# RMSNorm with each row repeated: another order of stores and loads on the DMA queue, wide copies, and the last tile undivided

## The chip, the core and the metric

The kernel runs on one core of a Trainium2 chip. The metric is the device time of one execution in microseconds (us), of which the median over several runs is taken. The kernel before took 240.07 us, the median of 5 runs between 239.79 and 240.6.

A core has several engines that run side by side, each with its own list of instructions. Four matter here: ScalarE (ACT in the profile), VectorE (DVE), GpSimd (POOL), and SyncE (SP), which here only issues transfers. All transfers between the large memory (HBM) and the on-chip memory (SBUF, 128 partitions) are carried by 16 DMA engines.

## What is computed

```python
def reference(x, gamma):            # x: (8, 512, 2048) f32, gamma: (2048,) f32
    x_rep = np.repeat(x, 2, axis=1)
    rms = np.sqrt((x_rep ** 2).mean(axis=-1, keepdims=True) + 1e-6)
    x_norm = x_rep / rms
    return (x_norm * gamma[None, None, :]).astype(np.float32)
```

Each of the 4096 rows is divided by the root of its mean square, multiplied by gamma and written out twice in succession. 33.55 MB are read and 67.11 MB are written.

## The kernel before, in words

The 4096 rows are cut into eight tiles of 512 rows (`ntiles` is 8). In a tile each of the 128 partitions holds `K = 4` successive input rows, which become 8 output rows. So a load is 4 MB (32 KB in each partition) and a store is 8 MB (64 KB in each partition), and both are contiguous in HBM within a partition.

**One buffer for input and output.** The buffer `y` of a tile has eight rows in each partition. The load (`load`, line 52) puts the four input rows into rows 4 to 7. Input row k is then scaled into row 2k, and a copy puts the same values into row 2k + 1. The pool `rows` has three such buffers, so tile i uses the buffer of tile i - 3, and load i cannot be issued until store i - 3 has landed.

**The work on a row.** `square` has ScalarE square the row and sum it up (line 64; the squares go to a throw-away tile in PSUM) and take the root (line 68). `scale` has VectorE take the reciprocal (line 73) and multiply the row by it and by gamma in one instruction (line 74). `repeat` copies one row (line 80). In `compute` the copies of all rows of a group but the last are ScalarE's, and that of the last row is VectorE's. On ScalarE the square of row k + 1 stands ahead of the copy of row k.

**The order of the work.** `tc.manual_schedule()` is entered: each engine's instructions stand in the order in which the program gives them. Every load and every store is issued by SP, which takes them one after the other and stands still at the first whose condition is not met. The order on SP is: load 0 in two halves, loads 1 and 2, stores 0 and 1, loads 3 and 4, stores 2 and 3, loads 5 and 6, stores 4 and 5, load 7 in two halves, store 6, store 7 in two halves. The last tile is both computed and stored by halves (`parts` in lines 108 to 111), and its load is halved as well (line 116).

**Gamma.** Four transfers of 2 KB, issued by ScalarE (line 98), bring gamma into one partition, and GpSimd copies it to all 128 (line 101). The first multiplication of line 74 needs that.

Of the kernel before, what the change touches and what calls it, by code (L numbers as in the profile page):

```python
# [1 line left out]

# [4 lines left out]


@with_exitstack
def kernel(  # L10
    ctx: ExitStack,
    tc: tile.TileContext,
    x: bass.AP,
    gamma: bass.AP,
    out: bass.AP,
):
    nc = tc.nc
    P = nc.NUM_PARTITIONS
    f32 = mybir.dt.float32
    Act = mybir.ActivationFunctionType  # L20
    Alu = mybir.AluOpType

    B, S, D = x.shape
    Bo, So, Do = out.shape
    R = So // S
    assert R == 2 and D == Do and B == Bo and So == S * R
    eps = 1e-6
    inv_d = 1.0 / float(D)


    K = 4
    N = B * S
    assert N % (P * K) == 0
    ntiles = N // (P * K)
    x_t = x.rearrange("b s d -> (b s) d").rearrange("(n p k) d -> n p k d", p=P, k=K)
    out_t = out.rearrange("b s d -> (b s) d").rearrange("(n p j) d -> n p (j d)", p=P, j=K * R)

    singles = ctx.enter_context(tc.tile_pool(name="singles", bufs=1))
    rows = ctx.enter_context(tc.tile_pool(name="rows", bufs=3))
    junk = ctx.enter_context(tc.tile_pool(name="junk", bufs=1, space=bass.MemoryType.PSUM))  # L40
    small = ctx.enter_context(tc.tile_pool(name="small", bufs=8))

    ys = []

    def load(i, eng, parts=1):


        y = rows.tile([P, K * R, D], f32, name="y")
        step = K // parts
        for k in range(0, K, step):  # L50
            at = K * (R - 1) + k
            eng.dma_start(out=y[:, at : at + step, :], in_=x_t[i, :, k : k + step, :])  # L52
        ys.append(y)

    def store(i, k0, k1):
        nc.sync.dma_start(  # L56
            out=out_t[i, :, R * k0 * D : R * k1 * D],
            in_=ys[i][:, R * k0 : R * k1, :].rearrange("p j d -> p (j d)"),
        )

    def square(i, k):
        sq = junk.tile([P, D], f32, name="sq")
        ss = small.tile([P, 1], f32, name="ss")
        nc.scalar.activation(  # L64
            out=sq[:], in_=ys[i][:, K * (R - 1) + k, :], func=Act.Square, accum_out=ss[:]
        )
        rms = small.tile([P, 1], f32, name="rms")
        nc.scalar.activation(out=rms[:], in_=ss[:], func=Act.Sqrt, scale=inv_d, bias=eps_t[:])  # L68
        return rms

    def scale(i, k, rms):
        rstd = small.tile([P, 1], f32, name="rstd")
        nc.vector.reciprocal(out=rstd[:], in_=rms[:])  # L73
        nc.vector.scalar_tensor_tensor(  # L74
            out=ys[i][:, R * k, :], in0=ys[i][:, K * (R - 1) + k, :], scalar=rstd[:], in1=gamma_b[:],
            op0=Alu.mult, op1=Alu.mult,
        )

    def repeat(i, k, copy):
        copy(out=ys[i][:, R * k + 1, :], in_=ys[i][:, R * k, :])  # L80

    def compute(i, k0, k1):

        rms = square(i, k0)
        for k in range(k0, k1):
            scale(i, k, rms)
            if k + 1 < k1:
                rms = square(i, k + 1)
                repeat(i, k, nc.scalar.copy)
            else:  # L90
                repeat(i, k, nc.vector.tensor_copy)


    ctx.enter_context(tc.manual_schedule())
    load(0, nc.sync, parts=2)
    gamma_b = singles.tile([P, D], f32, name="gamma_b")
    for c in range(0, D, D // 4):
        nc.scalar.dma_start(
            out=gamma_b[0:1, c : c + D // 4], in_=gamma[c : c + D // 4].partition_broadcast(1)
        )  # L100
    nc.gpsimd.partition_broadcast(out_ap=gamma_b[:], in_ap=gamma_b[0:1, :])  # L101
    eps_t = singles.tile([P, 1], f32, name="eps_t")
    nc.vector.memset(eps_t, eps)  # L103
    load(1, nc.sync)
    load(2, nc.sync)

    for i in range(ntiles):
        parts = 2 if i == ntiles - 1 else 1
        for k in range(0, K, K // parts):
            compute(i, k, k + K // parts)  # L110
            store(i, k, k + K // parts)

        if i % 2 == 1:
            for j in (i + 2, i + 3):
                if j < ntiles:
                    load(j, nc.sync, parts=2 if j + 1 == ntiles else 1)


# [1 line left out]
_INS = ['x', 'gamma']  # L120
_OUTS = [((8, 1024, 2048), 'float32')]


# [23 lines left out]
```

## Time and profile before

| | us |
|---|---|
| median of 5 runs | 240.07 |
| the profiled execution, its own time | 240.18 |
| its span, from the first instruction to the last | 238.4 |
| outside the span (the difference) | 1.78 |
| ScalarE busy | 115.4 |
| VectorE busy | 90.8 |
| GpSimd busy | 2.5 |

| line, engine, work | number | mean ns of one |
|---|---|---|
| 64, ACT, square of a row, 128x2048 | 32 | 1871 |
| 64, ACT, reading the sum | 32 | 187 |
| 68, ACT, root | 32 | 296 |
| 73, DVE, reciprocal | 32 | 162 |
| 74, DVE, row by reciprocal and gamma | 32 | 2352 |
| 80, ACT, copy of a row | 23 | 1890 |
| 80, DVE, copy of a row | 9 | 1227 |

Times within the profile are counted from the start of the span. A group's row gives the busy time of its instructions and the mean of one. The DMA share is the mean busy share of the 16 DMA engines in a stretch; since a packet is counted where it starts, a short stretch can show more than 1 or much less. The chain of waits is followed backwards from the end, from each step to what released it. An engine that is idle costs nothing as long as it is not the one that sets the end.

### The profile page before, as it was taken

The numbers are of one execution on the slowest core, as the hardware profiler recorded it, in microseconds if no ns is written. First come the engines' busy times: TensorE is split into PE (matmuls) and PEld (weight loads), VectorE is DVE, ScalarE is ACT, GpSimd is POOL, SyncE is SP. The second block draws the span as 40 slices with busy tenths as digits, with TensorE's granted clock in tenths as the row PEclk, the third lists the DMA queues.
The fourth block names the chain that finished last, engine by engine and source line by source line (L and its number), as shares of the span: only waits on it lengthen the run. The fifth ranks groups of instructions, "written<-read, shape, count | busy, mean of one in ns | idle before, by whom it ended". The sixth has DMA issues, their size and how long they took to land.

```text
span 238.4 us, 301 instructions
## 1 busy us (share of the span) xinstructions
DVE 90.8 (38%) x74; ACT 115.4 (48%) x121; POOL 2.5 (1%) x5
## 2 busy tenths in 40 slices
DVE  0086977864000085967000017796600019900000
ACT  2699999990000399996000059999400059600000
POOL 0300000000000000000000000000000000000000
DMA  7999998989899999989898999899998999898994
GB/s 265 438 443 440 440 440 352 528 352 528 352 440 418 423 418 447 495 363 517 352 528 352 440 440 507 374 462 418 418 462 363 426 426 533 363 506 363 434 429 203
DMA packets 2747, 100.69 MB, mean 422 GB/s; under 512 B 309, under 2 KB 309, under 8 KB 313
## 3 DMA queue, kind: packets, MB, share of 16 engines
q1 hardware_dynamic: 2736, 100.66, 98.4%
q14 instruction: 3, 0.02, 0.0%
q10 hardware_dynamic: 8, 0.01, 0.0%
HBM read 33.56 MB, written 67.11 MB: 422 GB/s over the span
## 4 chain that ended last, share of the span: by engine, by line
DMA 66%; ACT 14%; DVE 6%; issue 1%; SPq 0%; DVEq 0%
DMA out_dram<-y 40%; DMA y<-in_x_dram 25%; ACT sq L64 7%; ACT y L80 5%; DVE y L74 5%; ACT rms L68 1%; ACT L68 1%; DVE y L80 1%; DVE rstd L73 0%; SPq L52 0%; DVEq L74 0%; SPq L56 0%
## 5 line engine op out<-in xcount | busy, mean ns | idle before, releaser
L64 ACT ACTIVATE sq<-y 128x2048 f32<-128x2048 f32 x32 | 59.9, 1871 | 84.9 <-DMA y<-in_x_dram 84.9
L74 DVE SCALAR_TENSOR_TENSOR y<-y,rstd,gamma_b 128x2048 f32<-128x2048 f32 x32 | 75.3, 2352 | 1.2 <-DVE rstd L73 0.2
L73 DVE RECIPROCAL rstd<-rms 128x1 f32<-128x1 f32 x32 | 5.2, 162 | 115.8 <-ACT rms L68 115.8
L80 ACT COPY y<-y 128x2048 f32<-128x2048 f32 x23 | 43.5, 1890 | 3.7 <-DVE y L74 3.7
L80 DVE COPY y<-y 128x2048 f32<-128x2048 f32 x9 | 11.0, 1227 | 0.3
L68 ACT ACTIVATE rms<-ss,eps_t 128x1 f32<-128x1 f32 x32 | 9.5, 296 | 1.0
L64 ACT ACTIVATION_READ_ACCUMULATOR sq<-y 128x1 f32 x32 | 6.0, 187 | 0.0
L101 POOL PARTITION_BROADCAST gamma_b<-gamma_b x1 | 2.3, 2295 | 8.4 <-DMA gamma_b<-in_gamma_dram 8.4
L64 ACT ACT_TABLE_LOAD x1 | 1.3, 1283 | 2.1 <-issue 2.1
L68 ACT ACT_TABLE_LOAD x1 | 1.3, 1283 | 0.0
L103 DVE MEMSET eps_t<- 128x1 f32 x1 | 0.1, 59 | 0.8 <-PEq L131 0.8
L131 POOL MEMSET const-uint8-127<- 128x1 uint8 x1 | 0.1, 103 | 0.0
L131 POOL MEMSET const-bfloat16-1.0<- 128x1 bf16 x1 | 0.1, 102 | 0.0
L131 POOL MEMSET const-float32-0.0<- 128x1 f32 x1 | 0.1, 99 | 0.2 <-issue 0.2
L131 POOL MEMSET const-float32-1.0<- 128x1 f32 x1 | 0.1, 99 | 0.0
## 6 DMA issues: line engine op xcount, KB each, us to landing
y<-in_x_dram SPq DMA_DIRECT2D x6, 4096.0 KB, 25.0
y<-in_x_dram SPq DMA_DIRECT2D x4, 2048.0 KB, 9.6
out_dram<-y SPq DMA_DIRECT2D x2, 4096.0 KB, 27.0
out_dram<-y SPq DMA_DIRECT2D x7, 31.7
gamma_b<-in_gamma_dram ACTq DMA_DIRECT2D x4, 2.0 KB
```

Source lines behind the costliest of these rows:

```text
L64: nc.scalar.activation(out=sq[:], in_=ys[i][:, K * (R - 1) + k, :], func=Act.Square, accum_out=ss[:])
L68: nc.scalar.activation(out=rms[:], in_=ss[:], func=Act.Sqrt, scale=inv_d, bias=eps_t[:])
L73: nc.vector.reciprocal(out=rstd[:], in_=rms[:])
L74: nc.vector.scalar_tensor_tensor(out=ys[i][:, R * k, :], in0=ys[i][:, K * (R - 1) + k, :], scalar=rstd[:], in1=gamma_b[:], op0=Alu.mult, o ...
L80: copy(out=ys[i][:, R * k + 1, :], in_=ys[i][:, R * k, :])
L101: nc.gpsimd.partition_broadcast(out_ap=gamma_b[:], in_ap=gamma_b[0:1, :])
L103: nc.vector.memset(eps_t, eps)
L131: nc = _bacc.Bacc("TRN2", target_bir_lowering=False, num_devices=1)
```

## The change

The order on SP becomes: load 0 in two halves, loads 1 and 2, stores 0, 1 and 2, loads 3, 4 and 5, stores 3 and 4, loads 6 and 7, stores 5, 6 and 7. Load 7 and store 7 are undivided.

In a tile all four rows are squared and scaled before any copy. Then ScalarE copies the first two scaled rows in one instruction, and VectorE the last two in one instruction.

Gamma comes in seven pieces in place of four: one of 2 KB and six of 1 KB.

```diff
-    def repeat(i, k, copy):
-        copy(out=ys[i][:, R * k + 1, :], in_=ys[i][:, R * k, :])
+    def repeat(i, k0, k1, copy):
+        y_r = ys[i].rearrange("p (k r) d -> p k r d", r=R)
+        copy(out=y_r[:, k0:k1, 1, :], in_=y_r[:, k0:k1, 0, :])
 
-    def compute(i, k0, k1):
-
-        rms = square(i, k0)
-        for k in range(k0, k1):
-            scale(i, k, rms)
-            if k + 1 < k1:
-                rms = square(i, k + 1)
-                repeat(i, k, nc.scalar.copy)
-            else:
-                repeat(i, k, nc.vector.tensor_copy)
+    def compute(i):
+        for k in range(K):
+            scale(i, k, square(i, k))
+        repeat(i, 0, K // 2, nc.scalar.copy)
+        repeat(i, K // 2, K, nc.vector.tensor_copy)
...
-    for c in range(0, D, D // 4):
-        nc.scalar.dma_start(
-            out=gamma_b[0:1, c : c + D // 4], in_=gamma[c : c + D // 4].partition_broadcast(1)
-        )
+    cuts = [0, *range(D // 4, D + 1, D // 8)]
+    for c0, c1 in zip(cuts, cuts[1:]):
+        nc.scalar.dma_start(out=gamma_b[0:1, c0:c1], in_=gamma[c0:c1].partition_broadcast(1))
...
+    assert ntiles == 8
+    loads_after = {2: (3, 4, 5), 4: (6, 7)}
     for i in range(ntiles):
-        parts = 2 if i == ntiles - 1 else 1
-        for k in range(0, K, K // parts):
-            compute(i, k, k + K // parts)
-            store(i, k, k + K // parts)
-
-        if i % 2 == 1:
-            for j in (i + 2, i + 3):
-                if j < ntiles:
-                    load(j, nc.sync, parts=2 if j + 1 == ntiles else 1)
+        compute(i)
+        store(i, 0, K)
+        for j in loads_after.get(i, ()):
+            load(j, nc.sync)
```

## Prediction, made before the changed kernel was run

> **What bounds the kernel now.** I read the page's slices and its table of queues first, then stretches of the span, then the chain of waits, SP's own waits, and last the packet records behind them.
>
> ```profile
> DMA  7999998989899999989898999899998999898994
> GB/s 265 438 443 440 440 440 352 528 352 528 352 440 418 423 418 447 495 363 517 352 528 352 440 440 507 374 462 418 418 462 363 426 426 533 363 506 363 434 429 203
> ...
> q1 hardware_dynamic: 2736, 100.66, 98.4%
> ```
>
> The 16 DMA engines have work in every slice, and the packets of the one queue fill 98.4% of their time. Only the first and the last slice fall short.
>
> ```profile
> 2.00:26.00 24.00, 10.66 (x9) 18.45 (x18) 2.29 (x1) 1.00 1.01 430
> 26.00:34.00 8.00, 5.94 (x7) 7.50 (x11) 0.00 (x0) 1.00 1.03 393
> 56.00:80.00 24.00, 0.13 (x1) 0.00 (x0) 0.00 (x0) 1.00 1.01 437
> 80.00:110.00 30.00, 19.11 (x17) 27.36 (x30) 0.00 (x0) 1.00 1.01 437
> 140.00:170.00 30.00, 20.82 (x17) 28.50 (x30) 0.00 (x0) 1.00 1.01 435
> 218.00:235.00 17.00, 0.00 (x0) 0.00 (x0) 0.00 (x0) 1.00 1.00 434
> ```
>
> The last two columns are the DMA share and GB/s. The rate is 430 to 437 whether loads alone run (2 to 26 us), or stores alone (218 to 235), or both in turn (80 to 110), with the two computing engines busy or idle. The one low stretch is 26 to 34 us, at 393.
>
> ```profile
> 26.60 25.97 DMA out_dram<-y
> 52.57 0.02 issue
> 52.59 28.97 DMA y<-in_x_dram
> ```
>
> These steps of the chain (start, length, what) say how long a transfer is. Store 0 landed at 52.57, load 3 was issued at 52.59 and landed 28.97 us later, behind store 1: 12 MB, so 9.66 us for a load of 4 MB and 19.31 us for a store of 8 MB.
>
> ```profile
> SPq L56 <- DVE y L80: 121.4, 7, 30.2
> SPq L52 <- DMA out_dram<-y: 73.1, 5, 19.2
> ```
>
> SP waits long for copies and for landing stores, but the DMA share stays near 1 during these waits, since each time at least one transfer stands in the queue. So the bound is the DMA engines from the first packet (about 1.5 us) to the last (about 237 us). The packet records agree: between 2 and 234 us the 16 engines are hardly ever without a packet, in sum less than 0.1 us of their mean time. No order can buy what bubbles cost, as there are none. A change can win only what makes packets longer than they need be, or the unequal finish of the engines; it can lose by opening a bubble.
>
> **The transfers themselves.** A packet is one partition's share of a transfer. The records show 16 KB packets (halved loads, halved load 7) at 0.611 us, 32 KB packets (loads, halved store 7) at 1.213, and 64 KB packets (stores) at 2.418. Each engine carries 8 packets of every transfer. Before: 4 half loads give 32 x 0.611, 6 loads and 2 half stores 64 x 1.213, 7 stores 56 x 2.418, in sum 232.59 us. After: 16 x 0.611 + 56 x 1.213 + 64 x 2.418 = 232.46. That is **-0.13 us**. Two transfers fewer save two completion writes of 0.009 us: **-0.02**.
>
> By the Trainium skill, "DMA: Bandwidth & Descriptors", section "Anatomy of one DMA", a DMA has a fixed cost of some 2.0 us beside its bytes; 17 large transfers in place of 19 would by that be worth some 4 us, an estimate. The records show the next transfer's packets directly behind the last one's on the same engine, so that cost lies under the queue here, and only the very last landing shows it.
>
> **The turns from loading to storing, and the uneven finish.** Above the durations just given the packets took 1.81 us more per engine on average. Of this 0.66 us lies in the first 4 us, and 0.95 us between 28.9 and 32.7 us, on two packets of all 16 engines, right ahead of the first store; that is the 393 of the stretch. The rest, some 0.2 us on average, is uneven. The last engine lost 0.65 us at 146.3, 0.30 to an instruction fetch just before, and 0.53 at 196.5; it ended at 236.96, while the middle one ended near 235.6. Both places are just ahead of a turn from a load to a store. The change leaves three such turns (2 to 0, 5 to 3, 7 to 5) of four (2 to 0, 4 to 2, 6 to 4, 7 to 6), and one engine sets the end. The bounds are 0 (the turn at 90 us cost 0.01 on average) and -1.3 (the last engine's whole lag). On the other side another engine may catch a fetch and lose 0.5 more. I take **-0.25**, half of the 0.53 of one turn, since the lost turn need not be the dear one.
>
> **The computing, which lies under the transfers.** From this row to the next multiplication VectorE needs 2.47 us (multiplications start at 84.14 and 86.61), ScalarE 2.24 us a row for square and root (81.58 and 83.82). A tile after: the first multiplication starts 2.56 us after the first square (84.14 - 81.58), three more periods and the last multiplication, 3 x 2.47 + 2.35, bring it to 12.32. VectorE's copy of two rows is not in the trace; two single ones, 2.45, or, were it no faster than multiplying, 2 x 2.35 = 4.7. I take 2.45, by the row of the same operation. ScalarE's four squares end at 9.0 and its wide copy (2 x 1.89 at most) at 12.8, under VectorE. So a tile's store can go 14.8 us after its load landed (17.0 if the copy is slow), against 17.0 now (81.58 to 98.60). Per tile VectorE is busy 12.3 us and ScalarE 12.7, where the queue needs 29 us for its transfers: all of it is cover.
>
> The place with least cover is store 3. When load 3 lands, loads 4 and 5 stand behind it, 19.3 us; off that go some 0.5 us until ScalarE sees the landing and some 0.9 from the issue of a transfer to its first packet (0.72 to about 1.5 at the start, rounded up). That leaves 18 us for 14.8. **0**, with 3 us to spare. Load 4 and load 5 wait for stores 1 and 2 at places where two transfers stand in the queue; load 6 waits for store 3 with store 4 behind it, load 7 for store 4 with load 6 behind it. Stores 5, 6 and 7 have 19 us or more ahead of them. The first three stores: VectorE ends tile 0 at 12.15 + 9.76 + 2.45 = 24.4, tiles 1 and 2 by 37 and 49, while the queue holds transfers until 32, 51.6 and 71. **0**. The halved last tile is no loss either: load 7 will lie near 170 to 178 us, and its tile is ready some 20 us before its store's turn: **0**.
>
> Gamma: three more issues on ScalarE (262 ns in the middle, 513 at most) lie under the wait for load 0 until 8.19. On the wire its pieces went one by one between load packets, at 1.39, 5.41, 6.71 and 7.41 us, so 0.7 to 1.3 us for each of three more. The broadcast ends at 11.15 and is used at 12.15; the first multiplication would be 1.1 to 2.9 us later, and store 0 issued by 27.3 at most. The queue lasts until 32: **0**. At 4.0 us apiece, the widest spacing, store 0 would come at 35.4 and that cover would be gone, at a cost of about 4 us; that spacing was while the queue filled.
>
> **Sum.** 240.18 (profiled) - 0.13 - 0.02 - 0.25 = 239.78. The median of the runs is 0.11 under the profiled execution, so I say **239.7 us**.
>
> **Rivals.**
> First, the surplus goes: the 0.95 us ahead of the first store on all engines belongs to how that store is issued, and with store 0 coming about 2 us earlier or later it falls away; or the last engine's lag goes. With the 0.15 above that is 240.07 - 0.15 - 0.95 = **239.0**. For it speaks that no other turn cost so much; against it that the transfers up to that point are the same ones in the same order.
> Second, a bubble ahead of store 3, on the slower side. If the wide copies are held until all four multiplications are done and one copy is held by the other, store 3 goes at 12.32 + 3.78 + 2.45 = 18.55 us after landing, or with a slow copy 20.8, against the 18 of cover: 0.6 to 2.8 us of empty queue, in the middle **241.5**. It decides from 3 us of delay in the tile. Against it speaks that ScalarE's copy at 14.54 ran beside the multiplication of the next row at 14.61, so that rows of one buffer do not hold each other.
> Third, the finish becomes more uneven: a fetch and a slow packet (0.30 + 0.65) on the engine that is last already, 239.9 + 0.5 on average = **240.4**.
> That the order is not what it says can hardly be: SP takes its list in order, and there is one queue. Were the change no more than the moves that lie under the transfers, 240.0.
>
> **How the numbers follow.** The forecast 0.50, surplus gone 0.25, bubble 0.13, uneven finish 0.12. A measurement of this kernel can tell about 0.2%, 0.48 us, from no change, so no change is 239.59 to 240.55. The forecast lies near its lower edge: 0.38 of its chance within, 0.12 below. The surplus case is faster; the bubble is slower; the uneven finish is 0.07 within and 0.05 slower. Together faster 0.37, same 0.45, slower 0.18. The range goes from 238.9, the surplus case, up to 240.8, where it leaves out most of the bubble.
>
> **What would show it.** Right: the DMA share stays near 1 from 2 to 235 us, the stretch between the landing of load 5 and the first packets of store 3 included; a tile goes from its first square to its store in about 14.8 us; VectorE's wide copy takes about 2.4 us. Wrong: a slice near 115 to 120 us with a low share (bubble); a rate of 430 or more between 26 and 34 us (surplus gone); a last slice that is emptier with engines that end more than 1.3 us apart (uneven finish). A rate other than 430 to 437 while stores follow each other three at a time would upset the whole account.

## The result, and the profile after

The changed kernel took 239.46 us in the median of 20 runs (239.25 to 239.98), the kernel before 239.9 in the 38 runs beside them. The ratio is 0.9981, with a 95% interval of 0.9975 to 0.9987: 0.44 us faster. That lies inside the forecast range and just inside the 0.2% that had been called no change. The forecast of 239.7 stood on a kernel before of 240.07; as a gain it was 0.40 us.

The page of the changed kernel, its slices and its main queue:

```profile
DMA  7999998989999898999999998989998999989894
GB/s 265 437 447 441 441 441 353 520 364 474 408 419 463 353 529 353 441 441 436 436 463 430 421 463 353 529 353 441 436 502 386 474 408 419 463 386 496 353 529 176
...
q1 hardware_dynamic: 2448, 100.66, 98.6%
```

Nothing has changed in kind. The same 100.66 MB move in 288 packets fewer, and the packets of the one queue fill 98.6% of the DMA engines' time (98.4% before). The stretches (the last two columns are DMA share and GB/s):

```profile
2.00:26.00 24.00, 11.17 (x9) 17.70 (x19) 2.29 (x1) 1.00 1.00 430
26.00:34.00 8.00, 7.89 (x7) 7.90 (x10) 0.00 (x0) 1.00 1.05 393
56.00:80.00 24.00, 0.00 (x0) 0.00 (x0) 0.00 (x0) 1.00 1.01 437
...
116.00:122.00 6.00, 5.88 (x6) 5.93 (x7) 0.00 (x0) 1.00 1.02 437
...
218.00:235.00 17.00, 0.00 (x0) 0.00 (x0) 0.00 (x0) 1.00 1.00 432
```

Three stores in a row (56 to 80) run at the 437 of before, the stretch where store 3 takes over from load 5 (116 to 122) is full, and the one weak stretch, 26 to 34 us, is as weak as before: 393.

Where did 0.44 us come from? Not from the rate, and not from the mean engine. The packet records give the time at which each of the 16 engines made its last completion write:

| profile | mean of the 16 | last of the 16 | last behind the mean | span |
|---|---|---|---|---|
| before | 235.94 | 237.17 | 1.23 | 238.4 |
| after | 235.91 | 236.48 | 0.57 | 237.7 |

The mean engine finished 0.03 us earlier, the last one 0.69, and the span ended with the last one, 1.2 us behind it in both. The second-latest engine ended near 236.35 us in both, so what differs here is one engine of sixteen. These are two single executions, of 240.18 and 239.44 us, which lie further apart (0.74) than the medians (0.44). (The packet times in the prediction stood 0.22 us early: the first packet starts at 1.73, and the 236.96 given there is the 237.17 of the table.)

The timeline of tile 3, the place with least cover (start, length, engine, line):

```profile
101.26 1.88 ACT L64 ACTIVATE sq<-y 128x2048 f32<-128x2048 f32 x1 [53.17 <-DMA y<-in_x_dram]
...
103.83 2.35 DVE L74 SCALAR_TENSOR_TENSOR y<-y,rstd,gamma_b 128x2048 f32<-128x2048 f32 x1
...
111.21 2.35 DVE L74 SCALAR_TENSOR_TENSOR y<-y,rstd,gamma_b 128x2048 f32<-128x2048 f32 x1
113.60 2.29 DVE L81 COPY y<-y 128x4096 f32<-128x4096 f32 x1
...
115.96 0.34 SPq L56 DMA_DIRECT2D out_dram<-y  x1
```

From the first square to the issue of the store it is 14.70 us (14.8 in the prediction). The wide copies cost, by the groups of the page (busy time, mean ns):

```profile
L81 ACT COPY y<-y 128x4096 f32<-128x4096 f32 x8 | 28.7, 3592 | 1.4 <-DVE y L74 1.4
L81 DVE COPY y<-y 128x4096 f32<-128x4096 f32 x8 | 18.3, 2294 | 0.3
```

VectorE's copy of two rows that lie apart takes 2294 ns, against 2 x 1227: it is no slower per element than a copy of one row, and ScalarE's 3592 against 2 x 1890 likewise.

### The profile page after: what moved, and what is told of

The parts are those of the page before. It is cut to its first block, busy times and chain, and to the rows that moved or that the text cites. A ratio compares the mean times of both kernels' runs of the same rounds, so it can differ in the third digit from the quotient of the medians.

```text
span 237.7 us, 287 instructions
## 1 busy us (share of the span) xinstructions
DVE 96.5 (41%) x73; ACT 101.1 (43%) x106; POOL 2.5 (1%) x5
## 3 DMA queue, kind: packets, MB, share of 16 engines
q1 hardware_dynamic: 2448, 100.66, 98.6%
## 4 chain that ended last, share of the span: by engine, by line
DMA 58%; ACT 12%; DVE 9%; issue 1%; POOLq 1%; ACTq 1%; SPq 0%
DMA y<-in_x_dram 33%; DMA out_dram<-y 21%; ACT sq L64 8%; DVE y L74 7%; DMA gamma_b<-in_gamma_dram 4%; ACT y L81 3%; DVE y L81 2%; ACT rms L68 1%; POOLq L136 1%; ACTq L95 1%; DVE rstd L73 0%; POOLq L96 0%; SPq L56 0%
## 5 line engine op out<-in xcount | busy, mean ns | idle before, releaser
L81 ACT COPY y<-y 128x4096 f32<-128x4096 f32 x8 | 28.7, 3592 | 1.4 <-DVE y L74 1.4
L81 DVE COPY y<-y 128x4096 f32<-128x4096 f32 x8 | 18.3, 2294 | 0.3
L96 POOL PARTITION_BROADCAST gamma_b<-gamma_b x1 | 2.3, 2294 | 12.1 <-DMA y<-in_x_dram 12.1
```

Source lines behind the costliest of these rows:

```text
L81: copy(out=y_r[:, k0:k1, 1, :], in_=y_r[:, k0:k1, 0, :])
```

## The experiments

Theory A was the prediction's own: the transfers bound the kernel, and the gain is 0.15 us of packet durations and completion writes plus what the last engine no longer loses. Its rivals: B, shorter computing lets transfers go earlier; C, the undivided last tile gives all. Later came D and E, on why the order alone lost, and F and G, on what makes the last engine late. "Before" is the median of the kernel before, run on the same occasion. The ratio is an estimate from all runs and need not be the quotient of the two medians. The last columns are from one profile each, with the same meaning as in the table above, and "profiled" is the time of that one execution.

| kernel | us | before | ratio, 95% interval | profiled | mean | last | behind |
|---|---|---|---|---|---|---|---|
| order alone | 240.41 | 239.92 | 1.0032, 1.0016 to 1.0047 | 242.23 | 237.05 | 239.09 | 2.04 |
| wide copies alone | 240.00 | 239.92 | 1.0002, 0.9993 to 1.0011 | 240.16 | 235.99 | 237.15 | 1.16 |
| undivided last tile alone | 239.92 | 239.92 | 0.9998, 0.9986 to 1.0009 | 239.62 | 235.90 | 236.39 | 0.49 |
| gamma in seven alone | 240.27 | 239.92 | 1.0008, 0.9999 to 1.0016 | 240.32 | 235.95 | 237.22 | 1.26 |
| changed, last tile halved | 239.67 | 239.82 | 1.0000, 0.9992 to 1.0009 | 239.97 | 236.01 | 236.86 | 0.85 |
| changed, old computing | 239.65 | 239.82 | 0.9993, 0.9983 to 1.0002 | 239.56 | 235.95 | 236.61 | 0.66 |
| changed, old order | 240.00 | 239.82 | 1.0004, 0.9996 to 1.0013 | 240.04 | 236.00 | 237.10 | 1.10 |
| changed, gamma in four | 239.61 | 239.82 | 0.9995, 0.9986 to 1.0003 | 239.71 | 235.91 | 236.52 | 0.61 |
| changed, again | 239.67 | 240.35 | 0.9972, 0.9958 to 0.9985 | 239.70 | 235.87 | 236.75 | 0.88 |
| order alone, again | 240.74 | 240.35 | 1.0025, 1.0006 to 1.0045 | 241.76 | 237.06 | 238.62 | 1.55 |
| reciprocals on GpSimd | 249.50 | 240.35 | 1.0362, 1.0337 to 1.0387 | 249.50 | 245.16 | 246.54 | 1.38 |
| 640 memsets more | 242.74 | 240.23 | 1.0105, 1.0088 to 1.0122 | 243.20 | 237.02 | 240.23 | 3.21 |

### Each part alone on the kernel before

The order alone:

```diff
-        if i % 2 == 1:
-            for j in (i + 2, i + 3):
-                if j < ntiles:
-                    load(j, nc.sync, parts=2 if j + 1 == ntiles else 1)
+        for j in {2: (3, 4, 5), 4: (6, 7)}.get(i, ()):
+            load(j, nc.sync, parts=2 if j + 1 == ntiles else 1)
```

> The kernel before with the new order of stores and loads alone; the last tile stays halved, the copies and gamma as before. Theory A (the whole gain is in the DMA engines: 0.15 us of packet durations and completion writes from the undivided last tile, and about 0.3 us from the finish of the last engine, through one turn from loading to storing less): 0.3 us faster, 239.6 where the kernel before takes 239.9, and a last engine that ends less than 1 us behind the mean. Theory B (the shorter computing lets transfers go earlier): no difference, 239.9. Theory C (the undivided last tile gives all): no difference.

The wide copies alone (the middle of a group divides them, so that the halved last tile fits):

```diff
-        rms = square(i, k0)
+        mid = (k0 + k1) // 2
         for k in range(k0, k1):
-            scale(i, k, rms)
...
+            scale(i, k, square(i, k))
+        repeat(i, k0, mid, nc.scalar.copy)
+        repeat(i, mid, k1, nc.vector.tensor_copy)
```

> The kernel before with the squares and multiplications of a group ahead of its copies and the wide copies alone; order, halved last tile and gamma as before. Theory A: no difference, 239.9 within 0.15 us, though a tile goes from its first square to its store in 14.8 us in place of 17.0. Theory B: 0.4 us faster, 239.5. Theory C: no difference.

The undivided last tile alone:

```diff
-        parts = 2 if i == ntiles - 1 else 1
+        parts = 1
...
-                    load(j, nc.sync, parts=2 if j + 1 == ntiles else 1)
+                    load(j, nc.sync)
```

> The kernel before with load 7, the last tile's computing and store 7 undivided, nothing else changed. Theory A: 0.13 us from packets of 32 and 64 KB in place of 16 and 32 KB, and 0.02 from two completion writes less: 239.75. Theory C: 0.4 us faster, 239.5. Theory B: no difference. If the halving hid anything at the end, it would be slower: tile 7 is ready long before store 6 has gone, so no.

Gamma in seven pieces alone (the `cuts` of the change):

> The kernel before with gamma in seven pieces alone. All theories: no difference, 239.9 within 0.15 us; the first multiplication comes about 2.7 us later and store 0 is issued near 29 us, still ahead of the end of load 2 near 32. A bubble ahead of store 0, 0 to 0.5 us, would show that its cover is thinner than worked out.

Rival B falls: the wide copies alone bring store 0 to 24.13 us in place of 26.60 (line 56 in its timeline of SP: start and length of the merged issues), and the time stays at 1.0002.

```profile
24.13 13.53 SPq L56 DMA_DIRECT2D out_dram<-y  x2
```

Rival C is not what was measured either: 0.9998, though the interval still has room for the 0.15 us that theory A gave it. Gamma's pieces cost nothing clear of the noise.

The order alone was the surprise: 0.5 us slower, where theory A had 0.3 faster. In the profiled execution the last engine ended 2.04 us behind the mean, and the mean itself 1.1 us later than before. That execution was the slowest of twelve, 242.23 us against a median of 240.41.

### Each part taken out of the changed kernel

Four kernels, each with one part set back: the last tile halved again, the squares and single-row copies as before, `loads_after = {1: (3, 4), 3: (5, 6), 5: (7,)}`, and gamma in four pieces.

> The changed kernel with load 7, the last tile's computing and store 7 halved again. The order alone had been 0.5 us slower than the kernel before, with a halved load 7 that lies ahead of the turn to store 5 and with the old computing of 17.0 us a tile. Theory D (the old computing leaves too little ahead of store 3): this is 239.4 + 0.15 = 239.55, clearly under 239.9. Theory E (16 KB packets right ahead of the turn to storing are dear in the new order): as slow as the order alone, 240.2 or more, with slow 16 KB packets between 172 and 180 us.

> The changed kernel with the squares, multiplications and single-row copies of a tile as before (17.0 us from the first square to the store); order, undivided last tile and seven gamma pieces as changed. Theory D: as slow as the order alone, 240.2 to 240.4, with an empty queue or a fraction of a us of idle engines near 119 us. Theory E: 239.4 to 239.6.

> The changed kernel with the old order of stores and loads. My account (turns and finish, 0.25 of the 0.4): 239.7, halfway between the two kernels. If the order is worth nothing by itself and the undivided last tile and the wide copies are the gain: 239.45. Order alone having been slower, the new order may even cost: then under 239.4.

> The changed kernel with gamma in four pieces again: store 0 is issued 2.7 us earlier, load 2 at 2.3 us in place of 8.5. Gamma alone had been 0.08% slower, at the edge of its interval. If the seven pieces cost that: 239.25; if they cost nothing, 239.45 like the changed kernel.

With the three other parts in place the order does matter: the old order gives 1.0004, the new one 0.9981 and 0.9972. So the order is worth some 0.2 to 0.3% with the other parts and costs 0.25 to 0.32% without them. But the order is not alone in this. Each of the other three, set back, leaves a ratio (1.0000, 0.9993, 0.9995) whose interval reaches 1. The halved last tile takes the whole gain away, although the undivided one alone won nothing clear of the noise. A gain clear of the noise was measured only with all four parts together, and what a part is worth cannot be added up from the parts. (The changed kernel itself was run on other occasions than these four.) Neither D nor E explains the loss of the order alone: with the old computing and its 17.0 us a tile it is 0.9993, with the halved last tile 1.0000. With one of the three other parts old the new order is no slower than the kernel before; with all three old it is. Which two or three are needed was not tried.

Nor is it a bubble. In the order alone, SP issued store 3 at 118.06 us, 2.1 us later than in the changed kernel. Its timeline of SP (start, length of the merged issues, line) has stores 3 and 4 as

```profile
118.06 15.13 SPq L56 DMA_DIRECT2D out_dram<-y  x2
```

and the stretch around it, with DMA share and GB/s at the end, is full:

```profile
112.00:126.00 14.00, 10.41 (x10) 13.48 (x15) 0.00 (x0) 1.00 1.04 449
```

The changed kernel has the same 449 GB/s in this stretch:

```profile
112.00:126.00 14.00, 13.67 (x11) 13.87 (x14) 0.00 (x0) 1.00 1.04 449
```

What the profiled execution of the order alone lost lies in the packet records elsewhere: near 176 us, 3 us ahead of the turn from load 7 to store 5, all 16 engines lost 0.90 us on average on their 16 KB packets, and near 156 us some of them lost more, 0.25 on the average of all.

### Is either figure a matter of chance?

> The changed kernel itself, for comparison in this call and for a second profile. If its gain of 0.19% is real, 0.997 to 0.9987 of the kernel before again; three kernels that each undo one of its other parts stood at 0.9993 to 1.0000, so 0.9995 would mean that much of the gain was a matter of the chip or the hour.

> The new order alone on the kernel before, once more. If its 0.32% of loss belongs to the program: 1.002 to 1.005 again, with a second loss of about 0.9 us on all 16 engines near 176 us in the profile, ahead of the turn from the halved load 7 to store 5 (the first profile was of its slowest run). If it was a matter of the hour: 0.999 to 1.000, and one such loss in the profile like every other kernel.

Both came again, on another occasion: the changed kernel at 0.9972, the order alone at 1.0025, so the two ratios belong to the programs. The second profile of the order alone has the same losses in the same places (0.85 us near 176, 0.33 near 156). It too is of a slow execution, 241.76 us against a median of 240.74. So these losses go with executions that are 1.8 and 1.0 us above the median of their program; whether the half microsecond of the median comes from the same places is not shown.

### What makes the last engine late

In the first of two kernels GpSimd takes the reciprocals (`minus` is a column of -1.0).

```diff
-        nc.vector.reciprocal(out=rstd[:], in_=rms[:])
+        nc.gpsimd.tensor_tensor(out=rstd[:], in0=rms[:], in1=minus[:], op=Alu.pow)
```

> The changed kernel with the 32 reciprocals done by GpSimd (the root to the power -1) in place of VectorE. In all ten profiles so far an 8 KB packet of the instruction queue falls where VectorE has done 61 to 65 of its 90 to 94 listed instructions (134 to 147 us), and one DMA engine loses 0.3 us to it and 0.4 to 0.7 on its next packet; in most profiles that is the engine that ends last. Without the reciprocals VectorE's list is about 60. Theory F (that fetch makes the last engine late, and the last engine sets the time): one instruction packet less within the span, the last engine less than 0.45 us behind the mean in place of 0.6, and 0.3 to 0.5 us less than the changed kernel, 239.0. Rival G (the fetch only picks which engine is last; others are nearly as late): the same as the changed kernel within 0.15 us. GpSimd's path adds less than the 2.7 us that tile 3 has to spare; if more, a bubble near 119 us.

This did not test what it was made for. There were three instruction packets within the span instead of two, presumably because GpSimd's list had grown. GpSimd began its first power only at 26.89 us, and one power of 128 elements took 1466 ns on average. Its list of waits (who waited for what, us in total, times, longest) gives 11 us to nothing visible:

```profile
POOL rstd L73 <- issue: 11.0, 1, 11.0
```

And its stretches, with DMA share and GB/s at the end:

```profile
31.00:33.00 2.00, 2.00 (x2) 0.84 (x1) 1.53 (x1) 1.00 0.23 98
33.00:40.00 7.00, 6.35 (x4) 6.94 (x7) 1.57 (x1) 1.00 0.00 0
```

Store 0 went out at 39.30 us, and from 33 to 40 us not a byte moved. It is the bubble of the prediction's second rival at another place, with its price: in the packet records the DMA engines stood still for 8.0 us on average, and the kernel is 9.8 us slower than the changed one on the same occasion, with more lost at later turns.

The last kernel asks the question from the other side. It gives GpSimd, which is idle after the broadcast, 640 memsets for which nothing waits:

```diff
+    spare = singles.tile([P, 1], f32, name="spare")
+    for _ in range(640):
+        nc.gpsimd.memset(spare, 0.0)
     load(1, nc.sync)
```

> The changed kernel with 640 memsets of one element per partition on GpSimd, which has nothing else to do after the broadcast; nothing waits for them. They make its list longer, and so its instruction fetches: instructions of 64 bytes would be five more 8 KB packets in the instruction queue. Theory F (each such packet holds up one DMA engine by 0.3 us for itself and 0.4 to 0.7 on the next packet, and the transfers end with the last engine): if all five fall on one engine, it ends 1.5 to 4 us behind the mean and the time is 240.8 to 243, while the mean finish of the 16 engines moves by less than 0.3 us; if they spread over engines, under 0.7 us more. Rival G (the last engine's lag has to do with the turns alone): 239.5, as the changed kernel.

Theory F is borne out for fetches that pile up on one engine; rival G's 239.5 is not what was measured. Lines of its page: the memsets, and the queue of instruction fetches (packets, MB, share):

```profile
q14 instruction: 8, 0.06, 0.1%
...
L101 POOL MEMSET spare<- 128x1 f32 x640 | 71.2, 111 | 36.9
```

The stretches at the end of this kernel (DMA share and GB/s in the last columns):

```profile
235.00:237.00 2.00, 0.00 (x0) 0.00 (x0) 0.00 (x0) 1.00 0.15 66
237.00:241.40 4.40, 0.00 (x0) 0.00 (x0) 0.00 (x0) 1.00 0.03 15
```

After 237 us a single 64 KB packet was still started (4.40 us at 15 GB/s), on one engine. All five additional fetches, at 24.4, 48.2, 70.3, 90.2 and 110.1 us, fell on that engine, 0.31 us each, and the packet behind each took 0.09 to 0.35 more: 2.7 us in sum. At the end of the transfer ahead of the first of them the last engine lay 0.17 us behind the mean; at the ends of the transfers in which the five fell it lay 0.92, 1.24, 1.70, 2.15 and 2.82 us behind. It ended 3.21 us behind, and the median rose by 3.1 us against the changed kernel's 239.67 of the occasion before. Not all of that is the fetches'. The expected mean was missed: it rose by 1.1 us, as 16 engines lost 0.78 us near 176, ahead of the turn to store 5, as in the order alone. Of the 3.5 us between the profiled execution and that of the changed kernel run again, 2.3 are the greater lag of the last engine and 1.15 the later mean.

For the single fetch of the changed kernel the case is weaker. The engine that it falls on does end last, at 236.48, but the second-latest ended near 236.35, so that without the fetch that execution could have gained some 0.13 us.

## Why the prediction was right, and where its steps were off

**The bound** was right: DMA engines from first packet to last, both before and after. The work of the computing engines stayed hidden in every kernel but the one with the late powers.

**The packets, -0.13 and -0.02 us.** The packet durations were the same three (0.611, 1.213, 2.418 us), and the sum per engine is 232.46 as worked out, against 232.59. But the mean engine finished only 0.03 us earlier. Part of the rest is known: in the records a packet starts 3 to 4 ns ahead of the recorded end of the one before it, which the sum leaves out, and with 16 packets fewer on each engine that takes back some 0.05 us. Store 7 took 19.36 us in halves and 19.32 whole, from the mean completion of store 6 to its own. So the term was too large. A single part of this size cannot be told from no change by time: 0.9998 for the undivided tile alone. The 2.0 us a transfer that the prediction cites, and leaves out of its sum, stand in a section on transfers issued by GpSimd; those here are issued by SP, and two fewer of them moved the mean finish by 0.03 us, not by 4.

**The finish, -0.25 us.** By the profiles the place was right and the size a little small. Five profiles of the old order have a last engine 1.23, 1.16, 0.49, 1.26 and 1.10 us behind the mean, 1.05 on average; five of the new order with at least two of the other parts have 0.57, 0.88, 0.85, 0.66 and 0.61, 0.71 on average: 0.33 less. The last engine itself ended at 237.01 on average in the five old ones and at 236.64 in the five new ones, 0.36 earlier; 0.44 was measured between the medians. This is an indication, not a proof: they are single executions of different programs, the two groups overlap, and the smallest lag of all, 0.49, is in the old order. Since the first term came out smaller and this one larger than forecast, a total as near as 0.40 to 0.44 is in part luck. Two places carry the difference. The turn at 196 us, which the new order does not have, cost one engine 0.17 to 0.78 us in the five old ones; the last turn of the new order, near 177, cost 0.25 to 0.30 at most in four of its five (the fifth has the loss on all engines there). And the instruction fetch that by its place is taken to be VectorE's, which fell near 146 us just ahead of a turn and cost the next packet 0.58 to 0.65, falls near 134 amid stores (138 with the old computing) and costs 0.43 to 0.47.

**The reason given for it, fewer turns, was too simple.** It makes a term that belongs to the order alone, and the order alone has the same three turns and lost 0.5 us. The term is there only beside the other parts, and without the undivided last tile, which the sum counts apart, the gain was gone as well (1.0000). What the step overlooked is that a turn has no fixed price, 0.01 to 1.2 us per engine on average in these profiles, and that the parts of the change cannot be priced one by one.

**The computing at nothing** was right: 14.70 us for 14.8, 2.29 for 2.45. The cover ahead of store 3 was enough even for 17.0 us a tile, so the second rival was as unlikely as it was made.

**Gamma at nothing** was right too, with the delays as bounded: the first multiplication at 14.85 in place of 12.15, store 0 at 26.97, of at most 27.3. One thing was overlooked. In the timelines of the kernel before and of the changed kernel SP's first four load issues are

```profile
0.72 1.92 SPq L52 DMA_DIRECT2D y<-in_x_dram  x4
...
0.72 8.12 SPq L52 DMA_DIRECT2D y<-in_x_dram  x4
```

so they take 8.12 us in place of 1.92. SP's own waits in the changed kernel (us in total, times, longest) say why:

```profile
SPq L52 <- DMA y<-in_x_dram: 5.7, 1, 5.7
...
SPq L52 <- DMA gamma_b<-in_gamma_dram: 0.9, 1, 0.9
```

With seven transfers for gamma, SP stood 0.9 us for a piece of gamma before the second half of load 0, and 5.7 for the landing of its first half before loads 1 and 2, which went at 8.04 and 8.41. The second half of load 0 lay in the queue until 12.3 us, so this cost nothing, but it is a wait that nothing in the code shows.

**The first rival**, that the loss ahead of the first store would go, was wrong for this change: it is 1.1 us on all engines in the changed kernel (0.95 before), with store 0 only 0.4 us later. Where store 0 did come 2.8 us later, at 29.39 (gamma in seven alone), the stretch from 26 to 34 us carried 426 GB/s in place of 393, but as much was lost at later turns, and the kernel was no faster (1.0008). The third, a more uneven finish, happened where the order was changed alone.

**What stays open.** Why all 16 engines lose about 1 us some 3 us ahead of some turns, and not of others, was not found. Every profile has about 1 us of it, mostly ahead of the first store; where store 0 was issued at 29.4 us (seven gamma pieces with the old computing, two kernels) it came at later turns instead; the order alone and the kernel with 640 memsets have it twice. So why the order needs the other parts is shown as a fact and not explained.

## What to carry to other kernels

Where one queue keeps all DMA engines full, the time is that of the engine which ends last (in all fourteen profiles here the span ended 1.15 to 1.43 us behind it): compare the finish of the 16 engines before looking for a gain in order or computing. A shorter computing latency was worth nothing by itself here (1.0002), and changes of order must be measured together with the computing and the transfer sizes beside which they will run, as their value here changed its sign. The one bubble came when a tile was ready only after the queue ahead of its store had run empty; work that cover out in microseconds first, as it shows how far one can go. And before a profile is used to explain a median, see how far the profiled execution lies from it.

## What the runs showed of the hardware

- An instruction fetch was an 8 KB packet on a DMA engine and cost data transfers 0.31 us there and mostly 0.1 to 0.65 us on the next packet. 640 instructions more on GpSimd made five, all on one DMA engine: 2.7 us on that engine, in a kernel that became 3.1 us slower, though nothing waited for those instructions.
- Stores of 64 KB a partition move at 434 GB/s, loads of 32 KB at 432, of 16 KB at 429 (16 engines by the packet durations). Larger packets have little more to give.
- Ahead of a turn from loads to stores the engines lost between 0.01 and 1.2 us on average, in the same places in the two profiles of each program that was run twice.
- The first power on GpSimd began 11 us after the instruction ahead of it, with nothing in the profile that it waited for, and one of 128 elements took 1.47 us, where VectorE's reciprocal takes 0.16.
